# Reordering the first attention of block 2: keys first, half the queries and the output's first block between the attention's rounds

## The chip, the cores and the metric

The kernel runs on one core of a Trainium2 chip. The metric is the device time of one execution, in microseconds (us); lower is better. A profiled execution comes with a trace of every engine: PE (TensorE, matrix products; PEld is its weight load), DVE (VectorE), ACT (ScalarE), POOL (GpSimd) and SP (SyncE, whose queue issues the DMA transfers).

## The reference, cut to what matters

Two transformer blocks run one after the other on 256 tokens of width 1024. The second has two layers; each modulates its norms with vectors that come out of `cond @ w_ada`. The change lies in the first layer's mixer, a sparse attention with 16 query heads of 64 in 4 groups:

```python
q, kc, vc, ks, vs, kw, vw, gl = split(h @ w_in)          # 1024 | 6 x 256 | 48 columns
q = rms_norm(q, q_gain);  q_rot = rope(q)
gates = sigmoid(gl + b_gate)                             # (S, 16, 3)
k_cmp = rms_norm(compress(kc, pe_k, w_ck1, w_ck2));  v_cmp = compress(vc, pe_v, w_cv1, w_cv2)
o_cmp = masked_softmax(q . k_cmp) @ v_cmp                # 15 compressed positions
o_sel, o_win = the same with q_rot over (ks, vs) and (kw, vw)
y = (g0 * o_cmp + g1 * o_sel + g2 * o_win) @ w_out
x = x + g1_mod * y
...
```

With 256 tokens, selection and window both cover every causal position, so the kernel computes both as plain causal attention.

## The kernel before

All large products are done in three passes: each weight is split into a high and a low part (`whi` by ScalarE at L98, `wlo` by VectorE at L99), and so is each activation, and hi x hi, hi x lo and lo x hi are added in one PSUM bank. Weights come in tiles of 512 KB: `raw` (6 buffers), then `whi` and `wlo` (6 each). `tm_block` multiplies 512 columns of a weight with the normed input, 2 token halves x 8 k x 3 passes = 48 products; `fm_block` does 256 columns with the output transposed, also 48 products of 256 columns.

The program is written as Python, and a scheduler of the framework writes the order of each engine's queue: it walks a simulated timeline, takes what is ready by its place in the program, and hands out buffers as they come free. So the place in the program is a priority, not a fixed order; on TensorE pieces of a later step often stand between those of an earlier one. Each queue then runs strictly in the order written. Three helpers shape the program: `later(gen)` starts a generator and keeps it pending, `tick()` advances every pending one by a step, and `skewed(gens, fill)` starts one more generator per round, advances all live ones and calls `fill(r)`. `behind(e, ins)` orders an instruction behind the last one that was put into `fence[e]` for that engine: weight splits stand behind ScalarE's and VectorE's fence, the modulation products behind TensorE's.

The stage of this change, in program order before:

- `tm_block(w, 1024, ...)` makes the keys and values to be compressed; `emit_c` transposes them into `Z`.
- `q_block(0)`, `q_block(1)`: 8 heads each. `emit_q` norms, rotates, splits (VectorE and ScalarE), then transposes into `qT` and `qrT`.
- `compress()`: for keys and values 32 small products each of `Z` with two tiles `rawc` of `nsa_w_ck1` or `nsa_w_cv1`, fetched there by `cmp_weights` (L1147) into the pool `ad4`, then a hidden layer and `Bk`, `Vc`. `rescale()` works on GpSimd, `gate_block()` makes the gates.
- `kv_block(0)`, `kv_block(1)`: the other keys and values, into `kTd`, `kTl`, `vTM`; between them `cmp_probs(t)`, the compressed scores (L1348), their softmax and their transposes (L1369) into `PcT`.
- `wo`: the output weight's first 256 columns are split, the next two blocks fetched.
- The attention: 16 generators `att(p_, t)`, a pair of heads and a half of the tokens each. A round does the scores (L1394, L1397), maxima (L1401), exponentials (L1412) and scaling (L1418); two rounds later come the transposes (L1429), copied to `PT`, and one later the outputs (L1445, L1447), and after the second half `oT` by `hilo` (L215, L216), which is also the fence for ScalarE and VectorE. `fill` ticks and does one modulation step per round: `ada_step` loads a tile of `w_ada` (L427) into `ad4`, which has `B_N = 2` buffers, and multiplies it (L432, 8 products).
- `out_proj`: four blocks of 256 columns, each 48 products (L140 to L142), then the residual and the squares of the next norm.

PSUM has in this stage four banks for `mm` (scores, `tm`, `fm`, `cmp`), two for `ax` (transposes and small products), one for `acc` (the attention's output) and one for the modulation.

Of the kernel before, what the change touches and what calls it, by code (L numbers as in the profile page):

```python
# [19 lines left out]
P = 128  # L20
# [5 lines left out]
B_N = 2  # L26
# [12 lines left out]
def two_blocks_kernel(ctx, tc, A, out):  # L39
# [339 lines left out]
    def bc(a, shape):  # L379
        return a.to_broadcast([P] + shape)  # L380
# [770 lines left out]
    with ExitStack() as st2:  # L1151
# [4 lines left out]
        if True:  # L1156
# [39 lines left out]
            def q_block(n):  # L1196
# [19 lines left out]
                tm_block(w, 512 * n, hT, emit_q)  # L1216
# [18 lines left out]
            if True:  # L1235
# [23 lines left out]
                def compress():  # L1259
# [7 lines left out]
                    for kv, w1 in enumerate(("nsa_w_ck1_2", "nsa_w_cv1_2")):  # L1267
# [71 lines left out]
            def cmp_probs(t):  # L1339
# [5 lines left out]
                behind("V", V.tensor_scalar(al, al, 0.0, None, op0=OP.is_le))  # L1345
                ps = bank()
# [6 lines left out]
                V.tensor_tensor(sc_, ps[:, :256].rearrange("p (h n) -> p h n", h=16),  # L1353
                                bc(mb.unsqueeze(1), [16, 16]), op=OP.add)
                m = nw.tile([P, 16], F32, tag="cm", name="cm")
                V.reduce_max(m, sc_, axis=AX.X)
                V.tensor_tensor(sc_, sc_, bc(m.unsqueeze(2), [16, 16]), op=OP.subtract)
# [3 lines left out]
                V.tensor_tensor(m, m, gates[:, t, :, 0], op=OP.mult)  # L1361
                V.tensor_tensor(sc_, sc_, bc(al.unsqueeze(1), [16, 16]), op=OP.mult)
                V.tensor_tensor(sc_, sc_, bc(m.unsqueeze(2), [16, 16]), op=OP.mult)
                yield
# [3 lines left out]
                for j in range(4):  # L1368
                    T.transpose(pz[:, j * P:(j + 1) * P], scf[:, j * P:(j + 1) * P], ident)  # L1369
                V.tensor_copy(PcT[:, :, t * P:(t + 1) * P], pz.rearrange("p (j q) -> p j q", j=4))  # L1370
# [332 lines left out]
```

## Time and profile before

| | |
|---|---|
| median of 3 runs | 1252.32 us (1247.92 to 1252.46) |
| the profiled execution's own time | 1252.37 us |
| its span, first to last instruction | 1250.3 us |
| mean granted TensorE clock | 0.982 |
| TensorE busy in the span | 96% |
| VectorE busy | 71% |
| ScalarE busy | 56% |
| mean DMA rate | 206 GB/s |

The time is that of the whole execution; the span is what the trace covers. A busy TensorE is not one at its peak: products overlap in the pipeline and a product at half the clock is just as busy. So a stretch is read by how far apart its products start and by the granted clock, where 1.00 is 2.4 GHz and 0.50 is 1.2 GHz.

### The profile page before, as it was taken

The numbers are of one execution on the slowest core, as the hardware profiler recorded it, in microseconds if no ns is written. First come the engines' busy times: TensorE is split into PE (matmuls) and PEld (weight loads), VectorE is DVE, ScalarE is ACT, GpSimd is POOL, SyncE is SP. The second block draws the span as 40 slices with busy tenths as digits, with TensorE's granted clock in tenths as the row PEclk, the third lists the DMA queues.
The fourth block names the chain that finished last, engine by engine and source line by source line (L and its number), as shares of the span: only waits on it lengthen the run. The fifth ranks groups of instructions, "written<-read, shape, count | busy, mean of one in ns | idle before, by whom it ended". The sixth has DMA issues, their size and how long they took to land.

```text
span 1250.3 us, 22518 instructions
## 1 busy us (share of the span) xinstructions
PE 1200.8 (96%) x8762; PEld 1076.0 (86%) x8762; DVE 889.7 (71%) x1672; ACT 695.6 (56%) x1163; POOL 26.6 (2%) x34
## 2 busy tenths in 40 slices
PE   7999999999879999899999989999999989999998
PEld 6989999989657888778757879999977768999998
DVE  7999977664568999797767585477579666645443
ACT  6644447553357787566457455545556554655453
POOL 0000000000000000070000000000000000000000
PEclk9999999999989999999889989999999999999999
DMA  7665565791357999765451896597756335665551
GB/s 237 201 219 182 160 208 178 255 310 41 120 183 259 345 349 348 284 192 170 125 177 38 271 378 210 187 312 234 265 178 197 116 135 203 210 194 182 187 172 35
DMA packets 177551, 257.76 MB, mean 206 GB/s; under 512 B 14239, under 2 KB 138999, under 8 KB 177436
## 3 DMA queue, kind: packets, MB, share of 16 engines
q1 hardware_dynamic: 177436, 256.24, 62.0%
q8 instruction: 71, 1.16, 0.4%
q14 instruction: 44, 0.36, 0.1%
HBM read 255.15 MB, written 1.05 MB: 205 GB/s over the span
## 4 chain that ended last, share of the span: by engine, by line
PE 64%; DMA 3%; DVE 3%; ACT 1%; issue 1%; ACTq 0%; DVEq 0%
PE fm L141 6%; PE fm L140 6%; PE fm L142 6%; PE mo L140 5%; PE mo L141 5%; PE mo L142 5%; PE tm L147 3%; PE tm L149 3%; PE tm L148 3%; PE gu L149 2%; PE gu L147 2%; PE gu L148 2%; DMA ada<-in_w_ada_dram 2%; PE ada L432 1%; PE py L148 1%; PE py L149 1%
## 5 line engine op out<-in xcount | busy, mean ns | idle before, releaser
L99 DVE TENSOR_TENSOR wlo<-raw,whi 128x1024 fp32r<-128x1024 f32 (+1 forms) x382 | 455.6, 1216 | 178.5 <-ACT whi L98 177.2
L98 ACT ACTIVATE whi<-raw 128x1024 fp32r<-128x1024 f32 (+1 forms) x382 | 391.9, 1048 | 278.2 <-PE fm L141 148.8
L141 PE MATMUL fm<-hTl,whi 128*128 128x256 f32 (+1 forms) x968 | 277.6, 287 | 5.5 <-DVE hTl L216 4.5
L140 PE MATMUL fm<-hTh,whi 128*128 128x256 f32 (+1 forms) x968 | 276.8, 286 | 3.2 <-ACT hTh L215 3.2
L142 PE MATMUL fm<-hTh,wlo 128*128 128x256 f32 (+1 forms) x968 | 275.3, 285 | 0.0
L141 PEld LDWEIGHTS fm<-hTl,whi 128*128 128x128 f32 (+1 forms) x968 | 186.1, 192 | 7.8 <-DVE hTl L216 6.5
L140 PEld LDWEIGHTS fm<-hTh,whi 128*128 128x128 f32 (+1 forms) x968 | 186.0, 192 | 5.5 <-ACT hTh L215 4.6
L142 PEld LDWEIGHTS fm<-hTh,wlo 128*128 128x128 f32 (+1 forms) x968 | 186.0, 192 | 0.0
L141 PE MATMUL mo<-ul,whi 128*128 128x256 f32 x512 | 142.9, 280 | 0.0
L142 PE MATMUL mo<-uh,wlo 128*128 128x256 f32 x512 | 142.8, 280 | 0.0
L140 PE MATMUL mo<-uh,whi 128*128 128x256 f32 x512 | 141.7, 281 | 0.0
L141 PEld LDWEIGHTS mo<-ul,whi 128*128 128x128 f32 x512 | 96.3, 188 | 0.0
L142 PEld LDWEIGHTS mo<-uh,wlo 128*128 128x128 f32 x512 | 96.2, 188 | 0.0
L140 PEld LDWEIGHTS mo<-uh,whi 128*128 128x128 f32 x512 | 95.6, 188 | 0.4 <-issue 0.4
L147 PE MATMUL tm<-whi,hTh 128*128 128x512 f32 x176 | 70.0, 403 | 0.7 <-ACT hTh L215 0.7
L148 PE MATMUL tm<-wlo,hTh 128*128 128x512 f32 x176 | 69.4, 395 | 0.0
L149 PE MATMUL tm<-whi,hTl 128*128 128x512 f32 x176 | 68.5, 395 | 0.0
L141 PE MATMUL fm<-oTl,whi 128*128 128x256 f32 x192 | 55.0, 289 | 0.9 <-DVE oTl L1614 0.8
L140 PE MATMUL fm<-oTh,whi 128*128 128x256 f32 x192 | 53.9, 288 | 1.4 <-ACT oTh L1613 1.3
L142 PE MATMUL fm<-oTh,wlo 128*128 128x256 f32 x192 | 53.6, 283 | 0.0
L147 PE MATMUL gu<-whi,xgh 128*128 128x512 f32 x128 | 50.7, 398 | 2.0 <-ACT xgh L1011 2.0
L627 DVE SCALAR_TENSOR_TENSOR acv<-apad,chv,acv 128x256 f32<-128x256 f32 x120 | 51.6, 483 | 0.0
(523 smaller groups left out, 2150.9 us busy)
## 6 DMA issues: line engine op xcount, KB each, us to landing
ada<-in_w_ada_dram SPq DMA_DIRECT2D x96, 512.0 KB, 4.7
raw<-in_w_mlp_in_dram SPq DMA_DIRECT2D x64, 512.0 KB, 4.0
raw<-in_w_mlp_out_dram SPq DMA_DIRECT2D x64, 512.0 KB, 4.9
raw<-in_w_in_dram SPq DMA_DIRECT2D x48, 512.0 KB, 4.1
raw<-in_w_e_down_dram SPq DMA_DIRECT2D x32, 512.0 KB, 5.4
raw<-in_w_e_gate_dram SPq DMA_DIRECT2D x61, 256.0 KB, 4.9
raw<-in_w_e_up_dram SPq DMA_DIRECT2D x61, 256.0 KB
raw<-in_diff_w_in_dram SPq DMA_DIRECT2D x24, 512.0 KB, 3.9
```

Source lines behind the costliest of these rows:

```text
L98: behind("A", SC.activation(hi[:, :n], raw[:, :n], AF.Copy))
L99: last["lo"] = behind("V", V.tensor_tensor(lo[:, :n], raw[:, :n], hi[:, :n].bitcast(F32), op=OP.subtract))
L140: T.matmul(ps, whi[:, c:c + ncol], xh[:, xk, :], start=first, stop=False, **kw)
L141: T.matmul(ps, whi[:, c:c + ncol], xl[:, xk, :], start=False, stop=False, **kw)
L142: return T.matmul(ps, wlo[:, c:c + ncol], xh[:, xk, :], start=False, stop=last, **kw)
L147: T.matmul(ps, xh[:, xk, t0:t0 + P], w[0], start=first, stop=False)
L148: T.matmul(ps, xh[:, xk, t0:t0 + P], w[1], start=False, stop=False)
L149: return T.matmul(ps, xl[:, xk, t0:t0 + P], w[0], start=False, stop=last)
L432: behind("T", T.matmul(ada_part["ps"][32 * j:32 * j + 32, :], w, r[:, S * j:S * j + S], start=start, stop=stop, skip_group_check=True))
L627: V.scalar_tensor_tensor(acv[:, f, :], apad[:, f, j:j + S], chv[:, f, j:j + 1], acv[:, f, :], op0=OP.mult, op1=OP.add)
```

## The change

- The four `rawc` tiles are requested before `kv_block(0)`, and the pool `ad4` has 5 buffers (`B_N`). A smaller DMA scratch area makes room for them.
- Order: compressed keys, `kv_block(0)`, `compress()` and `rescale()` started, `kv_block(1)`, the masks, the first half of the queries, the weights `wq1` of the second half, `gate_block()`, `wo`. The second half of the queries' products (`q_pieces`) is cut into 8 pieces of 2 k: two ahead of the rounds, two in each of rounds 0 to 2.
- `cmp_probs` goes by halves of the heads, in rounds 0 and 5.
- Modulation: five tiles are loaded ahead of the rounds; from round 3 on one or two tiles are multiplied per round and one loaded.
- `out_first` does the output's first block in steps of one k (six products) in rounds 5, 7, ..., 17, in a bank `ps0` that is held; `out_proj` adds the last k.

```diff
-B_N = 2
+B_N = 5
...
-    def out_proj(aT, w2d, nx, gate=None, ws=(), ps0=None):
+    def out_proj(aT, w2d, nx, gate=None, ws=(), ps0=None, k0=6):
...
-                ps = out_first(aT, ws[0], KD, 6, ps0).rearrange("p (f q) -> p f q", f=2)
+                ps = out_first(aT, ws[0], KD, k0, ps0).rearrange("p (f q) -> p f q", f=2)
...
+            def q_pieces(n, wq):
+
+                emit = emit_qs(n)
+                for t in range(2):
+                    ps = bank("tm")
+                    for k in range(KD):
+                        fence["T"] = mm_tm(ps, hT, k, t * P, wq[k], k == 0, k == KD - 1)
+                        if k == KD - 1:
+                            later(emit(t, ps))
+                        if k % 2:
+                            yield
...
-                            r3 = cmp_weights(w1, half)
+                            r3 = rawc.pop(0)
...
-                q_block(0)
-                q_block(1)
-                later(compress())
-                later(rescale())
-                later(gate_block())
...
-            def cmp_probs(t):
+            def cmp_probs(t, hf):
...
-                for p_ in range(8):
-                    T.matmul(ps[:, p_ * 32:p_ * 32 + 32], qT[:, p_, t * P:(t + 1) * P], Bk[:, p_ // 2, :],
+                for j in range(4):
+                    p_ = 4 * hf + j
+                    T.matmul(ps[:, j * 32:j * 32 + 32], qT[:, p_, t * P:(t + 1) * P], Bk[:, p_ // 2, :],
                              start=True, stop=True)
-                Sc = nw.tile([P, 16, 32], F32, tag="s2", bufs=NS2, name="Sc")
+                Sc = nw.tile([P, 8, 32], F32, tag="s2", bufs=NS2, name="Sc")
...
+            rawc = [cmp_weights(w1, half) for w1 in ("nsa_w_ck1_2", "nsa_w_cv1_2") for half in range(2)]
             kv_block(0, 1536)
+            later(compress())
+            later(rescale())
+            kv_block(1, 2048)
             for t in range(2):
-                later(cmp_probs(t))
-            kv_block(1, 2048)
+                cmp_masks(t)
+            tm_block(w, 0, hT, emit_qs(0))
+            wq1 = wmat(w, KD, 512, 512)
+            later(gate_block())
             wo = [wmat(A["nsa_w_out_2"][0], KD, 0, 256)]
             wo += [wmat(A["nsa_w_out_2"][0], KD, 256 * c, 256, 0, 2) for c in (1, 2)]
-            tick()
-            tick()
-            ada_step(0, ad)
+            q1 = q_pieces(1, wq1)
+            for _ in range(2):
+                next(q1)
+                tick()
...
+            ps0 = []
+            ada_load(5, ad)
+
             def fill(r):
+
+                if r in (0, 5):
+                    for t in range(2):
+                        later(cmp_probs(t, r // 5))
+                for _ in range(2):
+                    next(q1, None)
                 tick()
-                if len(ada_todo) > 56:
-                    ada_step(1, ad)
+                if r >= 3:
+                    for _ in range(2 - (r % 3 > 0)):
+                        ada_mm(1)
+                        if len(ada_todo) > 56:
+                            ada_load(1, ad)
+                if r >= 5 and r % 2:
+                    p_ = (r - 5) // 2
+                    ps0[:] = [out_first(oT, wo[0], p_ + 1, p_, ps0[0] if ps0 else None)]
 
             skewed([att(p_, t) for p_ in range(8) for t in range(2)], fill)
+            while ada_ready:
+                ada_mm(1)
             drain()
     nx = norm(*adaln(0, 1, g_mlp0))
-    out_proj(oT, A["nsa_w_out_2"][0], nx, gate(0, 0), wo)
+    out_proj(oT, A["nsa_w_out_2"][0], nx, gate(0, 0), wo, ps0[0], 7)
...
-    nc = _bacc.Bacc("TRN2", target_bir_lowering=False, num_devices=1)
+    nc = _bacc.Bacc("TRN2", target_bir_lowering=False, num_devices=1, dynamic_dma_scratch_size=1024)
```

## Rows read from the trace of the kernel before

**Rows 1.** The head of the profile's page.

```profile
span 1250.3 us, 22518 instructions
```

**Rows 2.** Busy time by stretch: us, engines' busy us (records), clock, DMA share, GB/s.

```profile
535.50:579.80 44.30, 44.30 (x245) 37.74 (x242) 40.68 (x90) 32.70 (x60) 21.63 (x18) 1.00 0.66 204
579.80:590.00 10.20, 8.65 (x55) 7.75 (x54) 5.10 (x16) 4.26 (x10) 0.00 (x0) 0.83 0.57 168
590.00:613.00 23.00, 23.00 (x110) 17.86 (x109) 15.43 (x63) 12.87 (x31) 1.06 (x2) 1.00 0.36 115
613.00:630.40 17.40, 16.50 (x113) 10.78 (x112) 11.78 (x42) 4.67 (x12) 0.00 (x0) 0.65 0.55 157
630.40:644.80 14.40, 11.84 (x95) 6.85 (x94) 10.83 (x40) 8.84 (x37) 0.00 (x0) 0.95 0.63 189
644.80:681.90 37.10, 37.10 (x340) 26.09 (x339) 29.98 (x112) 26.31 (x108) 0.00 (x0) 1.00 0.26 82
681.90:693.40 11.50, 11.16 (x102) 8.92 (x101) 4.92 (x17) 4.76 (x14) 0.00 (x0) 1.00 0.05 7
693.40:713.90 20.50, 20.50 (x171) 20.50 (x172) 13.01 (x16) 8.96 (x11) 0.00 (x0) 1.00 1.01 357
```

**Rows 3.** The chain of waits, 535 to 720: start, us, what.

```profile
573.78 7.84 DMA rawc<-in_nsa_w_cv_dram
...
632.11 4.00 DMA ada<-in_w_ada_dram
...
636.86 4.55 DMA ada<-in_w_ada_dram
```

**Rows 4.** Who waited for whom, 520 to 720: total us, times, longest.

```profile
SPq L427 <- PE o L1445: 25.9, 1, 25.9
PE ada L432 <- DMA ada<-in_w_ada_dram: 3.3, 4, 1.7
PE cmp L1273 <- DMA rawc<-in_nsa_w_cv_dram: 1.6, 1, 1.6
PEld s L1394 <- ACT E L1412: 0.6, 2, 0.4
```

**Rows 5.** TensorE in order of time: start, us, line, operation, tiles, shape, count.

```profile
593.76 0.60 PE L1213 MATMUL ax<-ident,qn 128*128 128x128 f32 x4
594.11 0.48 PE L147 MATMUL tm<-whi,hTh 128*128 128x512 f32 x1
594.43 0.40 PE L148 MATMUL tm<-wlo,hTh 128*128 128x512 f32 x1
594.66 0.40 PE L149 MATMUL tm<-whi,hTl 128*128 128x512 f32 x1
...
653.10 0.64 PE L432 MATMUL ada<-ada,cond 128*32 128x256 f32 x8
...
670.17 0.39 PE L1394 MATMUL s<-kTd,qrT 128*128 128x256 f32 x1
...
676.01 0.38 PE L1394 MATMUL s<-kTd,qrT 128*128 128x256 f32 x1
```

**Rows 6.** VectorE in order of time, the same columns.

```profile
579.50 0.69 DVE L862 TENSOR_TENSOR qn<-tm,qgain 128x512 f32<-128x512 f32 x1
...
591.95 0.41 DVE L216 TENSOR_TENSOR qs<-qr,qs 128x256 fp32r<-128x256 f32 x1
...
616.09 0.42 DVE L1356 TENSOR_REDUCE cm<-Sc 128x16 f32<-128x256 f32 x1
...
693.86 3.50 DVE L99 TENSOR_TENSOR wlo<-raw,whi 128x1024 fp32r<-128x1024 f32 x3 [0.52 <-ACT whi L98]
```

**Rows 7.** ScalarE in order of time, the same columns.

```profile
679.45 0.37 ACT L1412 ACTIVATE E<-s,am 128x128 f32<-128x128 f32 x1 [0.99 <-DVE am L1402]
...
683.00 0.49 ACT L1412 ACTIVATE E<-s,am 128x256 f32<-128x256 f32 x1
...
692.77 5.79 ACT L98 ACTIVATE whi<-raw 128x1024 fp32r<-128x1024 f32 x6
```

More of the change, by code (lines that the diff above doesn't have):

```diff
@@ L1193, in kv_block, with emit_qs @@
                 tm_block(w, c0, hT, emit_k)
-            def q_block(n):
+            def emit_qs(n):
                 def emit_q(t, ps):
@@ L1266, in compress @@
                     nc.sync.dma_start(w2[:, 1, :], A["nsa_w_cv2_2"][0])
-                    for kv, w1 in enumerate(("nsa_w_ck1_2", "nsa_w_cv1_2")):
+                    for kv in range(2):
                         pc = bank("cmp")
                         for half in range(2):
-                            r3 = cmp_weights(w1, half)
+                            r3 = rawc.pop(0)
                             for k in range(8):
@@ L1329, in two_blocks_kernel, with cmp_masks @@
                     V.tensor_copy(Z[:, kv, 1024:1056:2], ps[:, :16])
-                q_block(0)
-                q_block(1)
-                later(compress())
-                later(rescale())
-                later(gate_block())
             PcT = npl.tile([P, 4, S], F32, name="PcT")
-            def cmp_probs(t):
+            cmask_ = {}
+            def cmp_masks(t):
                 al = nw.tile([P, 16], F32, tag="al", name="al")
@@ L1345, in cmp_probs @@
                 behind("V", V.tensor_scalar(al, al, 0.0, None, op0=OP.is_le))
+                cmask_[t] = (al, mb)
+            def cmp_probs(t, hf):
+                al, mb = cmask_[t]
                 ps = bank()
-                for p_ in range(8):
-                    T.matmul(ps[:, p_ * 32:p_ * 32 + 32], qT[:, p_, t * P:(t + 1) * P], Bk[:, p_ // 2, :],
+                for j in range(4):
+                    p_ = 4 * hf + j
+                    T.matmul(ps[:, j * 32:j * 32 + 32], qT[:, p_, t * P:(t + 1) * P], Bk[:, p_ // 2, :],
                              start=True, stop=True)
-                Sc = nw.tile([P, 16, 32], F32, tag="s2", bufs=NS2, name="Sc")
+                Sc = nw.tile([P, 8, 32], F32, tag="s2", bufs=NS2, name="Sc")
                 G.memset(Sc, 0.0)
                 sc_ = Sc[:, :, 0:16]
-                V.tensor_tensor(sc_, ps[:, :256].rearrange("p (h n) -> p h n", h=16),
-                                bc(mb.unsqueeze(1), [16, 16]), op=OP.add)
-                m = nw.tile([P, 16], F32, tag="cm", name="cm")
+                V.tensor_tensor(sc_, ps[:, :128].rearrange("p (h n) -> p h n", h=8),
+                                bc(mb.unsqueeze(1), [8, 16]), op=OP.add)
+                m = nw.tile([P, 8], F32, tag="cm", name="cm")
                 V.reduce_max(m, sc_, axis=AX.X)
-                V.tensor_tensor(sc_, sc_, bc(m.unsqueeze(2), [16, 16]), op=OP.subtract)
+                V.tensor_tensor(sc_, sc_, bc(m.unsqueeze(2), [8, 16]), op=OP.subtract)
                 SC.activation(sc_, sc_, AF.Exp, scale=0.125)
@@ L1360, in cmp_probs @@
                 V.reciprocal(m, m)
[L1361 to L1364, printed above, removed]
+                V.tensor_tensor(m, m, gates[:, t, 8 * hf:8 * hf + 8, 0], op=OP.mult)
+                V.tensor_tensor(sc_, sc_, bc(al.unsqueeze(1), [8, 16]), op=OP.mult)
+                V.tensor_tensor(sc_, sc_, bc(m.unsqueeze(2), [8, 16]), op=OP.mult)
                 yield
@@ L1367, in cmp_probs @@
                 scf = Sc.rearrange("p h n -> p (h n)")
-                for j in range(4):
+                for j in range(2):
                     T.transpose(pz[:, j * P:(j + 1) * P], scf[:, j * P:(j + 1) * P], ident)
-                V.tensor_copy(PcT[:, :, t * P:(t + 1) * P], pz.rearrange("p (j q) -> p j q", j=4))
+                V.tensor_copy(PcT[:, 2 * hf:2 * hf + 2, t * P:(t + 1) * P], pz[:, :S].rearrange("p (j q) -> p j q", j=2))
+            rawc = [cmp_weights(w1, half) for w1 in ("nsa_w_ck1_2", "nsa_w_cv1_2") for half in range(2)]
             kv_block(0, 1536)
+            later(compress())
+            later(rescale())
+            kv_block(1, 2048)
             for t in range(2):
-                later(cmp_probs(t))
-            kv_block(1, 2048)
+                cmp_masks(t)
+            tm_block(w, 0, hT, emit_qs(0))
+            wq1 = wmat(w, KD, 512, 512)
+            later(gate_block())
             wo = [wmat(A["nsa_w_out_2"][0], KD, 0, 256)]
             wo += [wmat(A["nsa_w_out_2"][0], KD, 256 * c, 256, 0, 2) for c in (1, 2)]
-            tick()
-            tick()
-            ada_step(0, ad)
+            q1 = q_pieces(1, wq1)
+            for _ in range(2):
+                next(q1)
+                tick()
             oT = act_pair("oT")
```

2 lines of the change are left out of this document (1 added, 1 removed).

## The prediction

> **What bounds the kernel now.** I read the stage by itself, since the change touches only block 2's first attention. The execution has a span of 1250.3 us [rows 1]; its own time is 1252.37 us, so 2.07 us lie around the span, and the median of the runs, 1252.32 us, is 0.05 us below it: no correction is needed. First view: the busy time by stretch [rows 2]. From the stage's first product (535.5) to the last of its output projection (713.9) are 178.4 us. TensorE shows work in nearly all of it; what changes is the granted clock: 0.83 in 579.8 to 590.0, 0.65 in 613.0 to 630.4, 0.95 in 630.4 to 644.8, otherwise 1.00. VectorE is busy 40.68 of 44.30 us in the first stretch and 29.98 of 37.10 us in the rounds: second in line. Second view: the chain of waits [rows 3]. In the weak stretches it runs through transfers: one of 7.84 us for the compression's weights and four for the modulation weights ("ada") between 617.9 and 641.5, two of which, of 4.00 and 4.55 us, stand in rows 3. Third view: the list of waits [rows 4]; TensorE itself stood 3.3 us for ada tiles and 1.6 us for rawc. Fourth: TensorE in order of time [rows 5], for the price of each product at full clock.
>
> **How much the stage loses.** At full clock a 512-column product starts 0.23 us after the one before, four transposes take 0.35 us and make the product behind them 0.09 us later (0.32 for 0.23), eight ada products take 0.64 us at most (0.57 to the next start), and a pair of rounds in mid-attention, from one first score to the next but one, 5.84 us [rows 5]. The output's 256-column products run at 20.50 us for 171, 0.12 us each [rows 2]. I counted TensorE's instructions in each weak stretch of rows 2 and priced them so.
> - 579.8 to 590.0: 32 compression products at about 0.11, three groups of four transposes at 0.45, 7.5 products at 0.23: 6.7 of 10.2 us. Lost 3.5.
> - 613.0 to 630.4: six ada tiles 3.4, 32 compressed-score products 3.7, eight of Vc 0.8, 16 key and 8 probability transposes 2.7: 10.6 of 17.4. Lost 6.8.
> - 630.4 to 644.8: five rounds' scores 4.5, 12 transposes 1.3, the first outputs 1.0, five ada tiles 2.9, two small transposes 0.3: 10.0 of 14.4. Lost 4.4. The stretch runs from the first scores to just past the first outputs: rounds 0 to 3 are latency, and only ada tiles stood in it.
>
> Together 14.7 us of 178.4; that is what the change can win here, apart from the ends.
>
> **The change, part by part.**
> (1) *rawc ahead of the first key block.* The four compression weights are requested before kv_block(0) instead of inside compress(). They are moved past the key block's weights on SP's queue, two of the four from about 574 to before 546. The cover is 48 products of 0.23 = 10.9 us; the longest chain transfer was 7.84 [rows 3]. DMA share there is 0.66 [rows 2]; 1 MB more in 44 us adds under a tenth. The 3.5 us of the first weak stretch go. Without that cover up to 7.84 us would come back behind the key block's weights.
> (2) *Keys first, second half of the queries last.* 48 products (10.9 us), their transposes (six groups of four, 2.7) and the compressed scores go into the rounds; attention starts earlier by what leaves the front. VectorE's sum: to the first score it does 40.68 + 5.10 + 15.43 + 11.78 = 73.0 us now [rows 2]; about 9 (the second half's norms, rotation and splits) and 6.5 (cmp_probs) leave. 57.5 us at the 0.92 share of the first stretch is 62.6 us: first scores at about 598 instead of 630.4. The half's emission takes 12.45 us from norm to split [rows 6]. While the first half's is under way TensorE has gate (2.8) and second half (10.9); while rounds 0 to 3 fill, it has the rest, 2.7 of transposes, 3.7 of compressed scores and the first ada tiles. By count this fills both holes; by order not wholly. Bounds: nothing of 11.2 us stays lost, or all does; I take 2.5, near the lower end, because the fill that is named (about 20 us) exceeds the 11.2.
> (3) *cmp_probs by halves*: the same 32 products, but 36 VectorE operations for 18. A full-width one is 0.42 us [rows 6]; at half width it costs between half and all of that, so VectorE gets 0 to 7 us more. It lies in rounds 0 to 5 under TensorE's fill. On the path: 0, and inside the bound of (2).
> (4) *Five ada buffers, loads ahead, products from round 3.* The four ada transfers of the chain [rows 3] come ahead of their products; the 3.3 us of waits [rows 4] are part of the 14.7. All 17 tiles (10 us) now lie in rounds 3 to 15, where six lay before round 0. What stands behind a waiting ada product on TensorE are the rounds' scores. The cover is five tiles of lead; without it rows 3 come back.
> (5) *The output's first block between the rounds.* 42 of its 48 products, 42 x 0.12 = 5.0 us, move ahead of the end. Before, some 20 of them (2.4 us) already ran as fill in the last rounds, 681.9 to 693.4 [rows 2]; now only the last 12 are that late, so 0 to 2 us of the tail open up: 0.8. What comes late next is the second block. Its weight halves wait for the last oT: ScalarE starts six at 692.77 just after it [rows 7], VectorE its first at 693.86, three in 3.50 [rows 6]. Before, the first block's rest hid them; now 0.72 us of products do. TensorE waits 0.5 to 2.3 us; the first VectorE half ends near 695.0 (693.86 + 3.50 / 3), the products before it at 693.4 + 0.7: 0.9, and 1.2 taken, as the second half follows 1.2 behind.
> (6) *Interleaving.* A change from transposes to products costs 0.09 us [rows 5], so about 0.2 us there and back; some 14 insertions (seven of six products, the rest query pieces): 0 to 2.8, taken at 1.4, as query transposes were interleaved before as well.
> (7) *One accumulator held.* ps0 keeps one of the four "mm" banks from round 5 to the end; a round's scores need two. Round by round: scores began at 676.01, its exponentials at 679.45 [rows 5, 7], two of them free the first bank at about 680.2, so a round holds it 4.1 us; the wider round behind it, with scores some 1.6 later, ended its exponentials at 683.5 [rows 7], 5.9 after its scores, and the second of the four about 1.2 before that: 4.7. With three banks a round may begin only when the last one's first bank is free: 4.4 us on the mean. TensorE's own pace in rounds 5 to 15 becomes (5.84 + 0.72 + 0.2 + 1.5 of ada) / 2 = 4.15 us. So 0 (latency shrinks, since ScalarE and VectorE wait less) to 11 x 0.25 = 2.8; taken at 1.0. The Trainium skill, PSUM — Partial Sum Buffer, Summary: rules for kernel authors, says to evacuate promptly, and its Perfetto Trace Analysis, Matmul Optimizations, to use all eight banks: both speak against this held bank. By that rule the round would be bank-paced, 2.8 us in the sum in place of 1.0, and 1246.4 us for the whole. With four banks the trace bears the rule out only faintly: scores waited 0.6 us in all for exponentials [rows 4].
> (8) The smaller DMA scratch only makes room; it issues nothing: 0.
>
> Sum: 14.7 - 2.5 - 0.8 - 1.2 - 1.4 - 1.0 = 7.8 us; 1252.37 - 7.8 = **1244.6 us**. What follows (norm, MLP) I leave as it is.
>
> **Rivals.**
> *More comes back (B).* SP's queue stood 25.9 us, until the last outputs, at the ada loads of the MLP [rows 4], and the weights behind them then came all at once: DMA share 1.01 in 693.4 to 713.9 [rows 2]. If five buffers let those loads go earlier, that rush spreads, and if the first rounds fill wholly, the costs of (2) and (7) vanish: 14.7 - 3.4 + about 2 = 13.3, 1239 us. Against it: TensorE does not wait in that stretch.
> *Only the transfers go (C).* The rounds' latency is a loop over VectorE and ScalarE; with the second half's emission and four cmp_probs in rounds 0 to 5 VectorE has 6 x 2.4 + 9 + 9 = 32 us there, near what TensorE has, and every dependence stretches. The eight work buffers are shared too: one emission holds four to five for 12 us. Then only 3.5 + 3.3 us are won, less 4.4: 2.4, 1250 us. That the scheduler puts the pieces back into blocks, so that the change does not do what it says, ends at about the same time.
> *Slower: the held bank decides (D).* Rounds 5 to 15 are paced by bank release. If the extra VectorE work stretches a round's 4.4 us to 5.6, eleven rounds lose (5.6 - 4.15) x 11 = 16.0 us in place of 1.0: 1252.37 - 8.8 + 16.0 = 1259.6 us. From (5.0 - 4.15) x 11 = 9 us, 5.0 us a round, it is slower than before. It is the page's rule of (7) in its strong form. For it: 81% of VectorE is taken already in the rounds [rows 2], and the compressed scores of the second half fall into round 5. Against: with TensorE fed otherwise, VectorE's share per round falls, as rounds get longer.
>
> **How the numbers follow.** Forecast 0.50 (its own range 1241 to 1248), B 0.15, C 0.22, D 0.13. 0.5% is 6.3 us, about what this kernel's measurement can tell from no change: the bounds are 1246.1 and 1258.6. Faster: 0.84 of the forecast and B, 0.57. Same: the forecast's rest, C, and that third of D which stays under 1258.6: 0.34. Slower: the rest of D, 0.09. The range takes the sum's bounds (14.2 us won at best; 14.7 - 11.2 - 2.0 - 2.3 - 2.8 - 2.8, a loss of 6.4, at worst) (1238.2 to 1258.8), B's side 2 us further down for what may follow the stage, and leaves out most of D: 1236 to 1257.
>
> **What would show it.** Right: no transfer in the chain of waits between 570 and 645; granted clock 1.00 through the stage's start; first scores near 600; the output's products between rounds; about 8 us less from 535.5 to the last output product. Steps: (5) shows as TensorE waiting about 1 us for a weight half after the last oT; (7) as scores waiting for ScalarE's exponentials. Wrong: rounds 5 to 15 further apart than 4.2 us; a new hole in rounds 0 to 4 with a granted clock under 1; key products waiting for weights behind rawc.

## The result, and the profile after

The changed kernel takes 1266.59 us (median of three runs, 1265.83 to 1271.69; a fourth, disturbed one of 1487.62 us at a mean granted clock of 0.742 is left out) against 1250.89 us (median of four) for the kernel before. The ratio is **1.0136, 95% interval 1.0103 to 1.0168**: slower by 1.4%, where 0.6% faster was forecast. The profiled execution took 1265.83 us. Its head line answers [rows 1]:

```profile
span 1263.6 us, 22526 instructions
```

From the stage's first product (537.71) to the last of its output projection (727.0) are 189.3 us, 10.9 more than before; 2.2 us are lost ahead of it, in code that is the same. The busy time by stretch, with the columns of [rows 2]:

```profile
537.70:557.80 20.10, 20.10 (x96) 16.71 (x93) 18.07 (x31) 15.87 (x29) 19.96 (x15) 1.00 1.00 303
557.80:580.80 23.00, 21.11 (x116) 18.26 (x114) 13.50 (x45) 8.81 (x20) 3.68 (x4) 0.85 0.50 151
580.80:608.10 27.30, 27.30 (x142) 22.63 (x142) 23.08 (x70) 16.57 (x33) 0.00 (x0) 1.00 0.57 178
608.10:620.00 11.90, 7.90 (x61) 6.32 (x60) 9.49 (x27) 7.13 (x20) 0.71 (x2) 1.00 0.14 44
620.00:636.40 16.40, 16.02 (x113) 10.99 (x112) 13.42 (x56) 8.85 (x30) 0.00 (x0) 1.00 0.41 129
636.40:640.00 3.60, 0.00 (x0) 0.00 (x0) 3.41 (x15) 1.57 (x5) 0.00 (x0) 1.00 0.00 0
640.00:664.70 24.70, 24.11 (x201) 17.11 (x201) 16.43 (x63) 14.57 (x54) 0.66 (x2) 0.93 0.39 126
664.70:708.00 43.30, 40.33 (x350) 28.69 (x350) 25.38 (x89) 21.80 (x82) 0.00 (x0) 1.00 0.35 122
708.00:727.00 19.00, 18.35 (x149) 17.95 (x150) 12.91 (x16) 8.74 (x11) 0.00 (x0) 1.00 0.64 204
```

Before, TensorE stood idle for 5.4 us of [rows 2]; the rest of what the weak stretches lost was clock and spacing. In the rows above it stands idle for 14.1 us: 8.7 of the 10.9 us are idle time. There are real holes: 4.0 us idle in 608.1 to 620.0, a whole 3.6 in which TensorE starts nothing while VectorE is busy for 3.41, and 3.0 in the rounds after 664.7. The list of waits, against [rows 4], has no transfer left in the stage; VectorE and ScalarE have taken their place:

```profile
PE ax L1213 <- DVE PT L1454: 3.7, 1, 3.7
...
PE ax L1213 <- DVE Vc L1332: 2.3, 1, 2.3
PEld s L1415 <- ACT E L1433: 2.0, 4, 1.0
...
PE cmp L1285 <- ACT Z L1269: 1.1, 1, 1.1
...
PE fm L142 <- DVE wlo L99: 0.7, 1, 0.7
```

So does the chain of waits, but for one ada transfer of 8.00 us at its end, from 699.22: at 564.41, where the chain of before ran through rawc [rows 3], it has the compression's products themselves, and at 639.29 VectorE's copy PT:

```profile
564.41 6.14 PE cmp L1285 x32
...
639.29 0.61 DVE PT L1454
```

TensorE in order of time, against [rows 5]: the compression, the first scores, the hole, one second score behind an exponential.

```profile
562.70 0.66 PE L1263 MATMUL ax<-ident,d 128*128 128x128 f32 x4 [0.83 <-DVE Z L1341]
564.41 6.14 PE L1285 MATMUL cmp<-Z,rawc 128*128 128x65 f32 x32 [1.06 <-ACT Z L1269]
570.31 0.77 PE L147 MATMUL tm<-whi,hTh 128*128 128x512 f32 x1
...
614.56 0.36 PE L1415 MATMUL s<-kTd,qrT 128*128 128x256 f32 x1
...
636.10 0.28 PE L1418 MATMUL s<-cmask,identb 128*128 128x256 bf16 x1
640.04 0.63 PE L1213 MATMUL ax<-ident,qn 128*128 128x128 f32 x4 [3.66 <-DVE PT L1454]
...
673.52 0.39 PE L1415 MATMUL s<-kTd,qrT 128*128 128x256 f32 x1 [0.78 <-ACT E L1433]
```

VectorE around the hole, as [rows 6] shows it for before:

```profile
634.15 0.68 DVE L862 TENSOR_TENSOR qn<-tm,qgain 128x512 f32<-128x512 f32 x1
...
637.55 0.69 DVE L864 TENSOR_TENSOR qn<-qn,ir_y 128x512 f32<-128x512 f32 x1
...
639.08 0.22 DVE L877 TENSOR_TENSOR qr<-ro 128x64 f32<-128x64 f32 x1
639.21 0.68 DVE L1454 COPY PT<-pz 128x512 f32<-128x512 f32 x1
```

The probabilities' transposes end by 634.8, but their copy PT stands behind the norm and the rotation of the second half's last tile, 634.15 to 639.2, in VectorE's order. TensorE's next transposes need the bank that PT empties, and everything behind them waits too. The Trainium skill's PSUM — Partial Sum Buffer, Engine vs sequencer instructions, says that VectorE's queue is strictly first in, first out; these rows agree, 3.66 us of it.

**What the stage loses, by parts.** I priced every product of the stage as in the prediction, at the start-to-start time that its form takes where nothing stands in front (0.23 us a 512-column product, 0.24 in the scores, 0.12 a 256-column one, 0.111 compression, 0.105 a transpose, 0.071 ada, 0.072 outputs), and subtracted that from each part's length. Every kernel below has the same products in its stage. These prices alone give 154.3 us for them; the work subtracted is 160.4 to 162.5 us, since a change from one kind of product to another also takes time (0.09 us behind four transposes [rows 5]), which no run prices by itself. So the losses are estimates, and their level is uncertain by some us. What can be read off is where the kernels, whose stages differ by 19 us, part from each other.

| | to the first scores | to the first outputs | to the last compressed output | to the end | sum |
|---|---|---|---|---|---|
| before | 9.9 | 4.5 | 1.4 | 0.7 | 16.5 |
| after | 10.3 | 1.4 | 14.1 | 2.1 | 27.9 |

### The profile page after: what moved, and what is told of

Its sections match the earlier page's. It is cut to its first block, busy times and chain, and to the rows that moved or that the text cites. A ratio compares the mean times of both kernels' runs of the same rounds, so it can differ in the third digit from the quotient of the medians.

```text
span 1263.6 us, 22526 instructions
## 1 busy us (share of the span) xinstructions
PE 1204.8 (95%) x8762; PEld 1078.6 (85%) x8762; DVE 893.3 (71%) x1690; ACT 696.2 (55%) x1165; POOL 28.9 (2%) x36
## 4 chain that ended last, share of the span: by engine, by line
PE 62%; DVE 5%; ACT 2%; DMA 1%; issue 1%; SPq 0%; ACTq 0%; DVEq 0%
PE fm L141 6%; PE fm L142 6%; PE fm L140 6%; PE mo L140 5%; PE mo L141 5%; PE mo L142 5%; PE tm L147 3%; PE tm L148 3%; PE tm L149 3%; PE gu L149 2%; PE gu L147 2%; PE gu L148 2%; DMA ada<-in_w_ada_dram 1%; PE ada L432 1%; PE s L1415 1%
```

## The experiments

Two theories stood at first. *Held bank*: from round 5 the rounds are paced by the release of score banks. *Front*: small holes at the start and up to the second half's queries, made by the order of the work. The stage is read from one execution; the same code ahead of it ends anywhere from 535.0 to 541.2 in these executions, so a verdict goes by the ratio, and the stage tells the place.

**noheld**: the output's first block whole behind the attention.

```diff
-                if r >= 5 and r % 2:
-                    ps0[:] = [out_first(oT, wo[0], p_ + 1, p_, ...)]
...
-    out_proj(oT, ..., wo, ps0[0], 7)
+    out_proj(oT, ..., wo)
```

> The changed kernel, but the output's first block goes back whole behind the attention: no accumulator bank is held from round 5 on, and no output products lie between the rounds. Theory 1 (the held bank sets the pace of rounds 5 to 15): pairs of rounds come down from 8.8 to 9.45 us to about 7.6 (8.3 by my count less 0.7 of output products), the waits of scores for exponentials go, and of the 18 us by which the change is slower some 8 to 10 come back even after the block's 5 us at the end: about 1260 us. Theory 2 (the front, before round 0 and up to the second half's queries, loses the time in small holes; the bank costs little): the products only move, within 2 us of 1269.

1261.7 us, ratio 1.0089 (1.0058 to 1.0120), stage 186.4. Some of it comes back, by the medians some 5 us, more than the 2 of the second theory and less than the 8 to 10 of the first; the two intervals still overlap a little.

The edit undoes more than the bank. Each call of `out_first` also moves TensorE's fence, and the ada products that come later in the program stand behind it. So in after only 4 of the 17 ada tiles run ahead of the block's first product, at 646.59, and none in the hole at 636; noheld runs all 17 from 626 to 652. The same stretch in after and in noheld:

```profile
626.00:655.00 29.00, 24.98 (x200) 16.97 (x202) 20.66 (x71) 19.02 (x68) 0.66 (x2) 0.94 0.37 116
```

```profile
626.00:655.00 29.00, 28.20 (x255) 15.32 (x255) 18.05 (x62) 17.41 (x62) 0.62 (x2) 1.00 0.67 227
```

The hole of 3.66 us is gone there:

```profile
643.24 0.66 PE L1213 MATMUL ax<-ident,qn 128*128 128x128 f32 x4
```

By the prices above noheld has nevertheless lost no less than after by 669 (it waits 1.91 us at 662.9). It gains in the rounds behind that, where TensorE is idle for 0.2 us from 668.9 to 700.9, and in after for 3.0 from 664.7 to 708.0.

**qfront**: the second half of the queries whole ahead of the attention.

```diff
-            q1 = q_pieces(1, wq1)
-            for _ in range(2): next(q1); tick()
+            tm_block(w, 512, hT, emit_qs(1), w=wq1)
```

> The changed kernel, but the second half of the queries is made whole ahead of the attention, behind the first half, instead of between the rounds. Theory 1 (held bank): rounds 5 to 15 stay as they are, 1269 within 3 us. Theory 2 (front): the hole of 3.66 us at 636.4 and the products at half clock behind it (some 1.5 us) go, and the 4 us of waits before the first scores are filled with the second half's 48 products (10.9 us); first scores come some 10 us later, at about 625, and the whole is 6 to 9 us shorter, 1260 to 1263.

1264.3 us, 1.0106 (1.0074 to 1.0137), stage 191.4, longer than in after although the time is shorter. The hole at 636 goes and comes again where the scores start, with VectorE and ScalarE on the same emission:

```profile
628.91 0.58 PE L1413 MATMUL s<-kTd,qrT 128*128 128x256 f32 x1 [4.57 <-ACT E L1431]
```

There the maxima of the scores are ready at 625.1. ScalarE has the emission's rotation and splits ahead of them in its order, stands 1.58 and 0.51 us for VectorE in these, and starts the exponentials at 628.07. 12.2 us are lost between first scores and first outputs (1.4 after), 8.2 behind them (14.1). The pieces as such are not the cause: the emission stands in the first rounds either way.

**cspread**: a `yield` behind each half of the compression: four groups of 16 products, as the trace counts them, for two of 32.

> The changed kernel, but the compression's 32 products come in four groups of eight, one behind each half of a block of 24 512-column products, instead of two groups of 16, of which both stood alone at 564.4 to 570.3. Theory 2 (front): the granted clock stays at 1.00 through 560 to 580 and 4 to 5 us come back: about 1264.5. Theory 1 (held bank): what comes back here waits in the rounds, 1269 within 2 us.

1263.95 us, 1.0121 (1.0080 to 1.0163), stage 188.9: not to be told from after. What comes back at 557 to 580 (about 2 us of 5.8) turns into a wait of 3.17 us for the compressed keys at 606.4, as the compression ends later.

**loads**: the kernel before with the transfers alone (and the smaller scratch).

```diff
-B_N = 2
+B_N = 5
...
+                rawc = [cmp_weights(w1, half) for w1 in ... for half in range(2)]
                 q_block(0)
...
-            ada_step(0, ad)
+            ada_load(5, ad)
...
-                if len(ada_todo) > 56:
-                    ada_step(1, ad)
+                ada_mm(1)
+                if len(ada_todo) > 56:
+                    ada_load(1, ad)
```

> The kernel before with the transfers of the change alone: five buffers for ada and rawc, rawc requested ahead of the queries, five ada tiles requested ahead of round 0, the smaller DMA scratch; every product stays in the order of before. If the transfers set the weak stretches of before (my step 4 and the first stretch), the 3.5 us of the first and at least the 3.3 us of ada waits go: 1244 us. If the loop over VectorE and ScalarE set them (my rival C): 1250, no change. If five buffers or the scratch cost the 2.2 us by which the changed kernel is late before the stage begins: 535.5 becomes about 537.7 here too, and the gain is less by that.

1246.65 us, **0.9965 (0.9948 to 0.9981)**, stage 174.1: it beats both kernels. The first weak stretch is at full clock. Of the 3.3 us of waits for ada tiles [rows 4] 1.7 are left. The stage starts at 535.6 here, but at 539.2 and 539.3 in two kernels below that have the same buffers, so what the 2.2 us ahead of it in after come from stays open:

```profile
577.00:590.00 13.00, 13.00 (x95) 12.08 (x93) 9.62 (x36) 8.10 (x18) 0.00 (x0) 1.00 0.69 233
```

**holdonly**: as noheld, but one of the block's eight parts runs in round 5 and takes the bank.

```diff
-                    ps0[:] = [out_first(oT, wo[0], p_ + 1, p_, ...)]
+                    if p_ == 0:
+                        ps0[:] = [out_first(oT, wo[0], 1)]
```

> The changed kernel, but of the output's first block only the first of its eight parts (six products of 256 columns) runs in round 5, which takes the accumulator bank; the other seven stay behind the attention. Against the kernel that gives the whole block back (noheld: stage 186.35 us, 1261.7 median) it differs by the held bank alone. Theory 1 (held bank): the waits of scores for exponentials come back, pairs of rounds from 8 onward are some 0.6 to 1.2 us longer than there, and the stage is 4 to 6 us longer: 191 us, 1266. Theory 2 (front): no more than 1 us between the two, 1262.

1264.94 us, 1.0117 (1.0100 to 1.0134), stage 189.2: 2.8 more than noheld, and the same as after. The edit does not single out the bank. The other seven parts stand behind the attention in the program, but as the bank is held five of them run between the rounds all the same, six products each from 658.2, 673.8, 681.7, 689.2 and 696.1. The fence moves in round 5 too: the hole of 3.66 us is back, at 634.8 to 638.4, ahead of the first product in the bank (645.71). From 669 on, past the last ada, scores start every 1.46 us in noheld (668.88 to 687.90, 14 products) and every 1.60 here (669.29 to 694.85, 17); but 18 output products, 2.2 us, stand between them here and none there, and without these it is 1.46 here too.

**late**: the block between the rounds only from round 11 (`r >= 11`).

> The changed kernel, but the output's first block begins in round 11 (with the first four of its parts at once) instead of round 5: all else as there, the same products between the rounds, the bank held for a third of the time. Theory 1 (held bank): rounds 5 to 10 lose none of the 0.35 to 0.6 us each, 2 to 4 us come back: 1265. Theory 2: the products fill less well, 0 to 1 us: 1269. A third: if the fill of products, not the bank, is what the rounds want, rounds 5 to 10 lose as much as with the bank.

1264.7 us, 1.0102 (1.0077 to 1.0126), stage 191.1: by the time between the two, by the stage none. Twelve ada tiles run ahead of the block here, and 1.0 us is left of the hole. It doesn't tell how the price depends on the rounds held.

**keysfirst**: loads with both key blocks and the compression ahead of both query blocks, whole; compressed scores one tile after the other.

```diff
-                q_block(0)
-                q_block(1)
+                kv_block(0, 1536)
+                kv_block(1, 2048)
                 later(compress())
...
-            kv_block(0, 1536)
-            for t in range(2): later(cmp_probs(t))
-            kv_block(1, 2048)
+            q_block(0)
+            q_block(1)
...
-            tick()
-            tick()
+            for t in range(2): tick(); tick(); later(cmp_probs(t))
```

> The kernel with the transfers alone (loads: 1246.7 median, stage 174.13 us), but keys first: both key blocks, then the compression, then both halves of the queries, whole; compressed scores of full width behind them, in the first rounds. No pieces between the rounds, no held bank. If keys first itself loses the time (the queries' emission on VectorE, 12.45 us from norm to split, stands last before the scores, where the key's shorter one stood), the first scores come no earlier than in loads (629.5) and the stage is 3 to 8 us longer than there. If only the pieces between the rounds and the compression's place lose it, the stage is within 1.5 us of 174.

1256.74 us, 1.0060 (1.0036 to 1.0084), stage 181.6. First scores come at 616.0, 13.4 us ahead of loads, against the expectation; then TensorE waits twice for a softmax that this edit put one behind the other:

```profile
638.46 1.09 PE L1370 MATMUL ax<-ident,Sc 128*128 128x128 f32 x4 [4.19 <-DVE Sc L1364]
...
646.46 1.09 PE L1370 MATMUL ax<-ident,Sc 128*128 128x128 f32 x4 [3.66 <-DVE Sc L1364]
```

**kfc**: keysfirst with both `cmp_probs` started together, their transposes a round behind.

> keysfirst (stage 181.57 us, 1256.7 median), with the compressed scores of both query tiles issued together and their transposes a round behind; there TensorE stood 4.19 and 3.66 us for the two softmaxes one after the other. If that order made its loss, 7 to 9 us come back: 173.5, 1248, level with loads: keys first by itself then costs nothing. If the first rounds are bound by VectorE (the emission of the queries stands there with the maxima, the scalings and the softmaxes), TensorE waits as long elsewhere and no more than 3 us come back: 179.

1252.39 us, 1.0019 (1.0003 to 1.0035), stage 173.9. By the stage keys first costs nothing against loads; by the ratio 0.5%, and the profiled execution loses that ahead of the stage (it starts at 537.8) and behind it. **kfc2**, with the ada tiles requested ahead of the output's weights and two products ahead of round 0, gave 1252.27 us, 1.0015 (1.0000 to 1.0031), stage 178.8 in the slowest of its twelve executions: by the time, nothing won.

> kfc (keys first, whole; stage 173.9 us, ratio 1.0019) with the ada tiles requested ahead of the output's weights and two of their products ahead of round 0. There 1.54, 0.48 and 0.69 us were waits for ada tiles. If those waits are the last thing that keeps TensorE there, 2 us come back: stage 172, ratio 1.000; if the emission on VectorE is, nothing.

**early**: loads with the ada tiles requested ahead of the output's weights and four products ahead of round 0.

> The kernel with the transfers alone (loads), but the five ada tiles are requested ahead of the output's weights on SP's queue, and four of the 17 ada products run before round 0, where loads still loses 3.4 us of 9.8 at 616 to 626 (it waits there 0.56 and 1.15 us for ada tiles). If TensorE lacks work in that stretch only because the tiles come late, about 2 us come back: 1244.5. If the stretch is a chain over VectorE and ScalarE that no fill shortens, what is filled there is missing in rounds 0 to 3 and the time stays at 1246.7 within 1 us.

1247.04 us, 0.9973 (0.9962 to 0.9984), stage 172.5: as loads.

**cafter**: noheld with the compression behind both key blocks.

```diff
-            later(compress())
-            later(rescale())
             kv_block(1, 2048)
+            later(compress())
+            later(rescale())
```

> noheld (the whole first output block behind the attention; stage 186.35 us, 1261.7 median), with the compression put behind both key blocks instead of behind the first. In every kernel with it behind the first block 5 to 6 us were lost at 556 to 580; with the compression behind two blocks of queries or of keys (loads, keysfirst) under 0.6. If the place alone makes that loss, 5 us come back in the stage: 181.5, 1257. If the compression's chain then comes late for Vc and the compressed scores, what is won there is lost before the first outputs: 186.

1258.48 us, 1.0066 (1.0041 to 1.0091), stage 184.5. The same 32 products now take 3.54 us to the next start:

```profile
571.34 3.79 PE L1285 MATMUL cmp<-Z,rawc 128*128 128x65 f32 x32
574.88 0.48 PE L147 MATMUL tm<-whi,hTh 128*128 128x512 f32 x1
```

against 5.9 in after. The part to the first scores loses 4.0 us instead of noheld's 10.6 (2.71 of the 4.0 are a wait for the compressed keys at 601.9), but 5.1 more are lost behind it.

**cyield** and **combo**: a second `yield` ahead of the compressed probabilities' transposes, in noheld and in cafter.

> noheld, with the transposes of the compressed probabilities one tick later in the order, a round behind their scores instead of in the same round. TensorE stood 1.91 us at 662.9 for the softmax of the second half there, and the scores behind it ran at half clock (3.6 us lost at 656 to 666). If the order is the cause, about 3 us come back: stage 183.4, 1258.7; if VectorE has no room for the softmax in any round, the wait moves a round on: 186.

> noheld with both of these edits. If they are two separate losses, 8 us come back: stage 178.4, 1253.7, level with the kernel before (1250) within 4 us, and still behind loads (174.1). If one takes the room of the other: 182, 1257.

cyield 1264.38 us, 1.0116 (1.0072 to 1.0159), stage 189.0: nothing, the lost time moves. combo 1255.08 us, 1.0043 (1.0021 to 1.0064), stage 180.4: with the compression out of the way something comes back.

**adafront** and **combo2**: in after and in combo, the five tiles requested ahead of `wo`, two ada products behind each of the two ticks ahead of round 0, one in each round from 0.

> The changed kernel (stage 189.3 us, 1269.1 median) with the 17 ada products where the kernel with the transfers alone has them: four ahead of round 0, then one a round from round 0, instead of all in rounds 3 to 15. If the holes at 608 to 618 and 636 to 640 (4.4 and 4.7 us lost) are for want of products that could stand there, 4 to 6 us come back: stage 184, 1264. If they are the latency of VectorE's emission and in-order waits, the ada products run in other holes and no more than 2 us come back.

> combo (no held bank, compression behind both key blocks, probabilities' transposes a round later; stage 180.4 us, ratio to before 1.0043) with the same move of the ada products. It lost 8.8 us at 597 to 618, before its first scores, where only query pieces could stand. If ada products fill that, 4 to 6 us come back: stage 175.5, ratio 0.9995, and every cause of the change's loss is then undone one by one; if not, 179 or more.

adafront 1263.78 us, 1.0115 (1.0086 to 1.0144), stage 187.4: the part to the first scores loses 7.2 instead of 10.3; the hole of 3.66 us stays, as ten tiles have run by then and the other seven stand behind the block's first product. combo2 1253.36 us, 1.0028 (1.0009 to 1.0047), stage 178.5: that part loses 0.9 instead of 4.7. Want of products, then, was the cause there; but of these 3.8 us the stage keeps 1.9.

**loadsheld** and **loadshold**: loads with the output's first block between the rounds, and with the bank held for one part alone (holdonly's edit).

> The kernel with the transfers alone (stage 174.1 us, ratio 0.9965) with the output's first block between the rounds from round 5 on, as the change has it: the held bank in the order of before. By noheld against holdonly a held bank costs 2.8 us of stage: 177, ratio 0.999. If the bank costs only where VectorE is loaded by the second half's emission, nothing: 174. If the fill it brings is worth more than the bank: 173.

> The kernel with the transfers alone, but one of the eight parts of the output's first block runs in round 5 and takes the accumulator bank; the other seven stay behind the attention. With all parts between the rounds (loadsheld) the stage was 182.3 us, ratio 1.0056; without any (loads) 174.1, 0.9965. If the bank is what costs: 180 to 183, ratio near 1.005. If the products between the rounds cost (their wait for the output's halves stands ahead of the next round in TensorE's order): 175, ratio 0.998.

loadsheld 1257.61 us, 1.0056 (1.0036 to 1.0076), stage 182.3; loadshold 1256.54 us, **1.0042 (1.0026 to 1.0058)**, stage 182.6. The held bank, with what goes with it, costs 8.4 us of stage and 0.77% of the time. As in holdonly, that isn't the bank alone: most of the block's other parts run between the rounds in loadshold too, so the two kernels are nearly one, and the fence holds back eleven ada tiles, which loads runs at 618 to 640, until 648.9. From the stage's start to the third group of the attention's outputs (647.01 in loads, 647.12 in loadshold) loadshold takes 3.6 us less, with 6.3 us of ada products (0.57 a tile) missing: 2.7 us are lost there, though the bank's first product starts only at 646.47. From there to the stage's end it takes 12.0 us more, 6.3 of them these tiles: 5.7 are left. TensorE shows no wait that explains them: it is idle for 1.1 us in that part and for 0.9 in loads, at a granted clock of 1.00 in both. What differs is the order, with 81 changes from one kind of product to another (transposes, scores, outputs, ada, projection) against 55; at 0.09 us each, the price of [rows 5], that would be 2.3 us, an estimate.

What the order shows is this. TensorE's scores of a narrow and a wide round, in loads and then in loadshold:

```profile
664.81 0.36 PE L1395 MATMUL s<-kTd,qrT 128*128 128x256 f32 x1
...
665.18 0.36 PE L1395 MATMUL s<-kTd,qrT 128*128 128x256 f32 x1
...
672.89 0.48 PE L1395 MATMUL s<-kTd,qrT 128*128 128x512 f32 x1
...
673.48 0.48 PE L1395 MATMUL s<-kTd,qrT 128*128 128x512 f32 x1
```

```profile
674.30 0.50 PE L1395 MATMUL s<-kTd,qrT 128*128 128x512 f32 x1
...
676.72 0.48 PE L1395 MATMUL s<-kTd,qrT 128*128 128x512 f32 x1
...
677.32 0.36 PE L1395 MATMUL s<-kTd,qrT 128*128 128x256 f32 x1
...
680.66 0.38 PE L1395 MATMUL s<-kTd,qrT 128*128 128x256 f32 x1
```

A round's two scores, 0.4 and 0.6 us apart with four banks, are 2.4 and 3.3 apart with three. VectorE's maxima of the wide round, and ScalarE's first exponential of it in answer to [rows 7], in loadshold:

```profile
675.41 0.68 DVE L1402 TENSOR_REDUCE am<-s 128x2 f32<-128x512 f32 x1
...
678.40 1.01 DVE L1402 TENSOR_REDUCE am<-s 128x2 f32<-128x512 f32 x2
...
679.33 0.16 DVE L1403 TENSOR_SCALAR am<-am 128x4 f32<-128x4 f32 x1
```

```profile
679.58 0.47 ACT L1413 ACTIVATE E<-s,am 128x256 f32<-128x256 f32 x1 [2.57 <-DVE am L1403]
```

L1403 scales the maxima of both scores at once, and no exponential starts before it. So with three banks the first score's bank is held, from 674.30, until the second score too has found a bank and been reduced; that the next round's score comes late for this bank is an inference, as TensorE has other products in the meantime. ScalarE's wait for the maxima in 640 to 710, in loads and in loadshold:

```profile
ACT E L1413 <- DVE am L1403: 4.5, 5, 1.3
```

```profile
ACT E L1413 <- DVE am L1403: 17.2, 10, 3.8
```

Two rounds (four scores) take 5.8 us in loads (13 products, 656.21 to 673.48) and 7.7 in loadshold (13, 668.65 to 691.70). But 20 output products, 6 ada products and 12 more of the attention's own outputs stand among the latter, 3.7 us by the prices above; without them it is some 6.4. What the bank costs by itself no run shows.

**qhalf**: combo2 in the old order: first half of the queries, then the keys, with the compression behind the first half and `kv_block(0)`.

> The last part by itself: the order of the kernel before (first half of the queries, then the keys, compression behind two blocks), transfers ahead, ada products from ahead of round 0, no held bank; the second half of the queries and of the compressed scores between the rounds. Against loads (stage 174.1 us, ratio 0.9965) it differs by that half's place and the width of the compressed scores. If the half's emission on VectorE stands in front of the first rounds' copies and softmaxes and costs as much as it fills, 176 to 180, ratio 1.001 or more; if the pieces fill the holes of the start, 171, ratio 0.994: the best of all.

1250.22 us, 0.9992 (0.9974 to 1.0010), stage 174.7: no faster than before; first scores come at 608.6, but 9.0 us are lost behind the first outputs (4.3 in loads).

**The stairs from after to loads.** Each line keeps what the line above undid and undoes more:

| kernel | undone besides | ratio to before | stage, us | lost in the four parts |
|---|---|---|---|---|
| after | - | 1.0136 | 189.3 | 10.3, 1.4, 14.1, 2.1 |
| noheld | bank held, block between rounds, ada behind its fence | 1.0089 | 186.4 | 10.6, 3.6, 10.1, 0.7 |
| cafter | compression behind one key block | 1.0066 | 184.5 | 4.0, 6.2, 12.3, 1.0 |
| combo | transposes in the softmax's round | 1.0043 | 180.4 | 4.7, 6.2, 8.1, 0.7 |
| combo2 | ada only from round 3 | 1.0028 | 178.5 | 0.9, 3.6, 11.3, 0.7 |
| qhalf | keys first | 0.9992 | 174.7 | 2.2, 2.0, 9.0, 0.7 |
| loads | second half of the queries in the rounds, halves of the compressed scores | 0.9965 | 174.1 | 6.5, 1.4, 4.3, 0.7 |

1.7% lie between the ends, far outside every interval. Single steps of 0.15 to 0.47% mostly do not, and they depend on what else is undone: the held block, with what goes with it, costs 0.3 to 0.5% here and 0.8 to 0.9% in the old order.

## Why the prediction was wrong

- **The loss that it set out from** was right: 14.7 us in three stretches, 16.5 over the whole stage by the finer count. What it held to be won came back elsewhere.
- **(1) rawc.** The transfer's 3.5 us do come back, in the old order (loads). In the change the step failed in its place: `compress()` moved with the keys, behind one key block instead of two query blocks. The copies of Z were not ready (0.83 and 1.06 us), and the 32 products ran at a granted clock of 0.57 (564.4 to 572.2). 5.8 us were lost at 557.8 to 580.8, where the old order lost 3.5 for the transfer.
- **(2) Keys first, half the queries in the rounds: the step that failed most.** VectorE's sum was right, 59.8 us of work before the first scores (57.5 foreseen); the share of 0.92 was not: it was 59.8 of 76.9, 0.78. VectorE stood too: 6.1 us for the key blocks' products and 3.0 for the compression's. First scores at 614.6, not 598. The 2.5 us "kept", on the strength of some 20 us of fill by count, are 4.4 in 608 to 618 and 6.4 in 628 to 648. The fill existed but stood elsewhere in TensorE's order: 13 of the 17 ada tiles behind the block's first product, by the fence that `out_first` moves, which the prediction left out. In the first rounds VectorE did the emission ahead of what TensorE was waiting for; where ada tiles stand in between (noheld), TensorE comes later and does not wait.
- **(3) Halves of the compressed scores** were priced at 0. noheld waits 1.91 us for the second half's softmax at 662.9; a later place for the transposes gives nothing there (cyield) and, by overlapping intervals, 0.2% once the compression is moved (combo). What the halves cost by themselves was not separated.
- **(4) Five buffers.** Right: no wait for a transfer, and the transfers by themselves (loads) 0.35% faster. That all ada products moved behind round 3 was seen, but not priced, and that most of them would stand behind round 5's output products was not seen: adafront gets 3.1 us of loss back before the first scores.
- **(5) The tail** was right: 0.65 us for a weight half, 0.47 for the last oT, 1.4 us more lost than before; 2.0 foreseen.
- **(6) Interleaving**, 1.4 us, was not measured by itself. loadsheld against loadshold can't show it, as the block's parts run between the rounds in both. The 5.7 us that no wait explains may be in part of this kind.
- **(7) The held bank.** The mean pace was foreseen, 4.4 us a round (the rounds from 673.52, 682.43 and 691.88 are 8.9 and 9.45 us apart in pairs), and the sign shows: scores wait 0.8 us for exponentials on TensorE, 2.0 in its weight loads (0.6 before [rows 4]). The price, 1.0, can't be held against a measurement of the bank alone. Bank, insertions and displaced ada tiles together cost 2.8 to 3.0 us of stage here and 8.4 in the old order, against 2.4 for (6) and (7). I had added up how long a bank is held in a kernel with four. With three, a round's two scores come apart, and as the maxima are scaled together each then holds its bank longer. By the Trainium skill's PSUM — Partial Sum Buffer, Summary: rules for kernel authors, banks should be evacuated promptly; loadshold, which holds one, is 0.8% slower than loads, but no run separates that rule from the change of order.
- **The rivals.** The slower side happened, but not by D alone: the held block, with all that goes with it, is about a third of the loss of 1.4% (noheld). C, the loop over VectorE and ScalarE, had the right place for most of the rest, yet only as far as no change: new holes were in none of the rivals.

Three things stay open: what the held bank costs by itself, why the held block costs less in the new order than in the old, and keys first taken whole (kfc), which costs 0.5% by the time and nothing by the stage of its one execution.

## What to carry to other kernels

Fill counts only where it stands in the engine's order: ask of every hole which instruction is next in the queue, and of a moved block what it takes away from where it stood. An edit that holds a bank can move a fence too: count in the trace which products changed place before a cause gets the price. Where one instruction joins two banks (here the scaling of both maxima), losing one of four can split the pair. Try the part that only moves transfers by itself: here it was the whole gain.

## What was not expected of the hardware

The same 32 products of 65 columns took 5.9 us where two waits of 0.83 and 1.06 us stood in front of them, at a granted clock of 0.57 to 572.2, most of it at the lower level of 1.2 GHz; behind 512-column products without a wait they took 3.54 us, with the clock at 1.00. Behind the two waits, 1.9 us together, these products alone took 2.4 us longer.
